# Weight tiles at other distances from the activations: one distance for the last feed-forward layer, a test series in the first, four in turn in the attention and the delta rule

## The chip, the cores and the metric

The program runs on one core of one Trainium2 chip. The metric is the device time of one execution in microseconds (us); 2737.4 us is the median of three runs of the kernel before. Where a profile is read, its times are those of one further execution, taken with the hardware profiler.

TensorE multiplies a stationary operand, which a weight load (LDWEIGHTS, the row PEld of the profile) puts into the array, with a moving operand that is streamed from SBUF. VectorE is DVE in the profile, ScalarE is ACT, GpSimd is POOL, and SP is the queue from which the weights' DMAs are issued.

## The reference

A trunk of two layers over 256 tokens of width 2048, all in float32:

```python
x = x + diff_attention(rms_norm(x, mixer_norm[0]), ...)   # 8 heads, two softmax maps a head
x = x + conv_ffn(rms_norm(x, ffn_norm[0]), ...)           # layer 0
x = x + gated_deltanet(rms_norm(x, mixer_norm[1]), ...)   # 16 q/k heads, 32 v heads, chunks of 64
x = x + conv_ffn(rms_norm(x, ffn_norm[1]), ...)           # layer 1

def conv_ffn(h, w_up, conv_w, conv_b, w_down):            # width 5504 = 43 * 128
    u = causal_dwconv(h @ w_up, conv_w) + conv_b
    val, gate = jnp.split(u, 2, axis=-1)
    return (jax.nn.silu(gate) * val) @ w_down
```

Nearly all arithmetic is in the projections: `h @ w_qkv` and `@ w_o` of the attention, `h @ w_in` and `@ w_out` of the delta rule, `h @ w_up` and `@ w_down` of the two feed-forward layers.

## The kernel before

**One projection.** Activations lie transposed in SBUF, 128 features by 256 tokens a tile, each as two parts (a rounded part and the rest, `a[:, 0]` and `a[:, 1]`), so that three products in the fast fp32r format stand for one in float32. `dense` (L98 to L118) computes one *block*: 256 output features over all `kt` input tiles. It takes the weights in chunks of four input tiles. `weights` (L77 to L90) brings a chunk by a DMA from SP's queue (`raw`), rounds it on ScalarE (`whi`, L88) and takes the rest on VectorE (`wlo`, L89). For each input tile and each half of the block, three matmuls follow at L115, L116 and L117: the stationary operand is 128 columns of `whi`, of `wlo`, of `whi` again, and the moving operand is a tile of 256 tokens. A block with 16 input tiles (`w_qk`, `w_o`, `w_up`, `w_in`) is 96 matmuls, one of `w_down` with 43 tiles is 258, one of `w_out` with 8 tiles is 48. `raw`, `whi` and `wlo` have three buffers each. `dense_tok` (L125) is the other form, with the weights as the moving operand, for `w_v` and `w_z`; the change leaves it as it is.

**The distance.** A buffer of `whi` or `wlo` is 128 elements longer than its data. `dense` starts the data `(place - x) % 128` elements into the buffer, where `place` stands for the activations' own position (HP, AP or OP) and `x` is an entry of `dist`, the first for `whi` and the second for `wlo`. So `x` is a distance between the addresses of moving and stationary operand, counted in elements of 4 bytes modulo 512 bytes: 51 is 204 bytes. Nothing but these addresses depends on `dist`. The default is (51, 51).

**Order.** The stages run one after the other: the attention (16 blocks `w_qk`, a query and a key block for each head; 4 of `w_v`; 8 of `w_o`), the feed-forward layer 0 (43 blocks `w_up`, then 8 of `w_down`), the delta rule (a gate block; four batches of heads, each with four "k" blocks, one "v" block, two of `w_z` and three "v" blocks; the eight `w_out` blocks of a batch come one batch later), and the feed-forward layer 1. TensorE works through the blocks in program order. In the mixers, `tick` (called after every chunk) puts the small matmuls of the attention and of the delta rule (tiles `mp`) between those of the projections; in the feed-forward layers only the norm's matmuls stand between them, in the first `w_up` block.

**Distances before.** The feed-forward layers hold series, block by block. `w_up` of layer 0 goes through 0 to 42, that of layer 1 through 43 to 63 and then through eleven pairs, 51 and one of 0, 16, 24, 32, 8, 4, 48, 60, 12, 36 and 51. `w_down` has pairs for `whi` and `wlo`, as the diff shows. All other projections have 51.

Of the kernel before, what the change touches and what calls it, by code (L numbers as in the profile page):

```python
# [19 lines left out]
KD = D // P  # L20
EPS = 1e-6
CK = 4
HP, AP, OP = 40, 48, 112
LNEXP = "natural_log_exp_and_others"


class Trunk:
# [38 lines left out]
    def mp(self):  # L66
        return self.mps.tile([P, 512], F32, tag="mp", name="mp")
# [9 lines left out]
    def weights(self, ap, d=(0, 0)):  # L77
# [4 lines left out]
        def tile_(tag, dt, bufs, room=0, d=0):  # L82
            t = self.wp.tile([P, CK * T + room], dt, tag=tag, name=tag, bufs=bufs)
            return t[:, d:d + nk * n].rearrange("p (k n) -> p k n", n=n)
# [15 lines left out]
    def dense(self, w, kt, acts, place, tiles=2, lead=0, dist=(51, 51)):  # L100
# [3 lines left out]
        ps = self.banks()  # L104
        for k0, nk in self.chunks(kt, CK, lead):
            hi, lo = self.weights(w[:, k0:k0 + nk, :], [(place - x) % P for x in dist])
# [18 lines left out]
    def dense_tok(self, w, kt, acts):  # L125

        nc = self.nc
        ps = self.banks()
        for k0, nk in self.chunks(kt, CK // 2):
            hi, lo = self.weights(w[:, k0:k0 + nk, :], (HP, HP))  # L130
# [118 lines left out]
    def ffn(self, w_up, w_down, nj, cols_ap, done, final=False):  # L249

        nc = self.nc
        self.spawn(self.norm_stat())
        with self.tc.tile_pool(name="fp", bufs=1) as fp:
            cols = fp.tile([P, 8 * nj + 64], F32, tag="fcols", name="fcols")[:, :8 * nj]
            cols = cols.rearrange("p (t h j) -> p t h j", t=4, h=2)
            nc.scalar.dma_start(cols, cols_ap)
            acts = []
            one = [(r, r) for r in range(64)]
            if final:
                ups = one[43:] + [one[r] for i in range(11) for r in (51, (0, 16, 24, 32, 8, 4, 48, 60, 12, 36, 51)[i])]  # L260
                downs = [(51, 51), (48, 48), (51, 19), (51, 35), (19, 51), (35, 51), (16, 51), (51, 16)]
            else:
                ups = one[:43]
                downs = [(51, 51), (51, 48), (48, 51), (51, 50), (51, 52), (51, 0), (48, 0), (51, 32)]
            rows = self.rows(fp.tile([P, nj * 2 * T + 8], F32R, tag="ac", name="ac"), nj, 0)
            for j in range(nj):
                ps = self.dense(w_up[j], KD, self.h_acts, HP, dist=ups[j])
                c = []
                u = fp.tile([P, 2, T], F32, tag="u", name="u", bufs=2)
                self.merge(ps, u)  # L270
                for half in range(2):
                    o = fp.tile([P, T], F32, tag=f"cv{half}", name="cv", bufs=2)
                    c4 = [cols[:, t, half, j:j + 1] for t in range(4)]
                    self.conv(o, u[:, half, :], c4[:3], c4[3])
                    c.append(o)
                nc.scalar.activation(c[1], c[1], AF.Silu)
                a = c[0]
                nc.vector.tensor_tensor(a, c[0], c[1], ALU.mult)
                ac = rows[j]
                self.split(ac, a)  # L280
                acts.append(ac)
            self.project(w_down, nj, lambda k: acts[k], AP, done, final, downs)

    def attention(self, w_qk, w_v, w_o, nh, dist_ap, ident_ap, qg, kg, lvec, sub, start, done, lambda_init):

        nc, mp = self.nc, self.mp
        with self.tc.tile_pool(name="at", bufs=1) as at:
            self.spawn(self.norm_stat(3))
            qgs = at.tile([P, 1], F32, tag="qgs", name="qgs")
# [3 lines left out]
            dist = at.tile([P, 384 + 72], F32, tag="dist", name="dist")[:, :384]  # L293
# [21 lines left out]
            def squares(r):  # L315
                sq = at.tile([P, 2, T], F32, tag="sq", name="sq", bufs=2)
                nc.scalar.square(sq, r)
                sp = at.tile([P, 2, 2, T], F32R, tag="sqp", name="sqp", bufs=3)
                self.split(sp, sq)
                return sp  # L320

            def normed(ps, gain):
                r = at.tile([P, 2, T], F32, tag="qkr", name="qkr", bufs=3)
                self.merge(ps, r)
                sq = squares(r)
                qn = at.tile([P, 2, T], F32, tag="qkn", name="qkn", bufs=4)

                def go():
                    yield
                    pn = mp()  # L330
                    self.total(pn, [sq])
                    ri = at.tile([P, 2, T], F32, tag="ri", name="ri", bufs=2)
                    self.rsqrt(ri, pn, P)
                    nc.vector.scalar_tensor_tensor(qn, r, gain, ri, ALU.mult, ALU.mult)

                return qn, go()
# [57 lines left out]
            aTs = []  # L394
            for h in range(nh):
                acts, lead = (self.h_acts, 0) if h else (start, 1)
                qn, go = normed(self.dense(w_qk[h], KD, acts, HP, lead=lead), qgs)
                self.spawn(go)
                kn, go = normed(self.dense(w_qk[nh + h], KD, self.h_acts, HP), kg)
                aT = at.tile([P, 384], F32, tag=f"aT{h}", name="aT")  # L400
                self.spawn(weigh(h, qn, kn, go, aT))
                aTs.append(aT)
# [14 lines left out]
    def gdn(self, w_gate, w_in, w_z, w_out, nb, hb, gate_ap, const_ap, hot_ap, conv_col, ng, done):  # L417
# [8 lines left out]
        nq = nb * hb  # L426
# [3 lines left out]
        with tc.tile_pool(name="gd", bufs=1) as gd:  # L430
# [20 lines left out]
            def lin(ps):  # L451
                u = gd.tile([P, 2, T], F32, tag="u", name="u", bufs=2)
                self.merge(ps, u)
                return u

            def convs(u, tiles):
                c = gd.tile([P, 2, T], F32, tag="cv", name="cv", bufs=4)
                for i in range(2):
                    self.conv(c[:, i, :], u[:, i, :], [conv_col(t, tiles[i]) for t in range(4)], None)
                nc.scalar.activation(c, c, AF.Silu)  # L460
                return c
# [204 lines left out]

            def out(b, acts):
                for blk in range(KD // 2):
                    ps = self.dense(w_out[b * (KD // 2) + blk], 2 * hb, lambda k: self.await_(acts, k), OP)
                    self.add_out(blk, ps, done if b == nb - 1 else None)  # L670

            pg = self.dense(w_gate, KD, self.h_acts, HP, tiles=1)
# [1 line left out]
            pend = None  # L674
            for b in range(nb):
                heads = range(b * hb, (b + 1) * hb)
                cc = gd.tile([P, 32, 32], F32, tag="s4", name="Cc", bufs=3)
                nc.gpsimd.memset(cc, 0.0)
                lqs, inv, acts, zts, vts = [], [], [], {}, {}
                groups = [range(i, i + gh) for i in range(0, hb, gh)]  # L680
                plan = [("k", i) for i in range(hb)] + [("v", 0)] + [("z", g) for g in range(len(groups))]
                for op, i in plan + [("v", i) for i in range(1, hb)]:
                    if op == "k":
                        hq = heads[i]
                        c = convs(lin(self.dense(w_in[hq * 2], KD, self.h_acts, HP)), (hq, nq + hq))
                        self.spawn(keys(hq, c, cc, 2 * i, lqs))
                        if i == hb - 1:
                            self.spawn(invert(cc, lqs, inv))
                    elif op == "z":
                        gr = groups[i]  # L690
                        zt = zts[i] = gd.tile([P, 2, gv, P], F32, tag="vz", name="zt", bufs=4)
                        ps = self.dense_tok(w_z[heads[gr[0]] // 2], KD, self.h_acts)
                        for t in range(2):
                            nc.scalar.activation(zt[:, t].rearrange(flat), ps[:, t, :], AF.Silu,
                                                 scale=self.rstdc[:, t:t + 1])
                    else:
                        gi = i // gh
                        gr = groups[gi]
                        if i == gr[0]:
                            vt = gd.tile([P, 2, gv, P], F32, tag="vz", name="vt", bufs=4)  # L700
                            ready = []
                            self.spawn(group(gi, gr, lqs, inv, vt, ready, zts, acts))
                        hq = heads[i]
                        c = convs(lin(self.dense(w_in[hq * 2 + 1], KD, self.h_acts, HP)),
                                  (2 * nq + 2 * hq, 2 * nq + 2 * hq + 1))
                        self.spawn(to_tokens(c, vt, 2 * (i - gr[0]), ready))
                if pend:
                    out(*pend)
                pend = (b, acts)
            out(*pend)  # L710

    def gates(self, gd, pg, nv, gp, ident, triu, res):
# [132 lines left out]
def trunk_kernel(tc, a, out):  # L845
    nc = tc.nc
    with ExitStack() as ctx:
# [3 lines left out]
        nc.sync.dma_start(cols[:, :KD], a["cols"][:, :KD])  # L851
        parts = t.chunks(KD, CK, 1)

# [58 lines left out]
```

## Time and profile before

| | |
|---|---|
| median of 3 runs (lowest, highest) | 2737.4 us (2737.03, 2738.95) |
| the profiled execution's own time | 2739.05 us |
| its span, first to last instruction | 2737.3 us |
| granted TensorE clock | 0.999 |
| `w_up` / `w_down` of layer 0 | 490.21 / 239.07 us |
| `w_up` / `w_down` of layer 1 | 483.28 / 240.51 us |
| attention's `w_qk` blocks with what lies between | 207.07 us |
| delta rule with `w_out` | 876.18 us |

How to read it: the stages' times are stretches of the span, cut where the first matmul of a stage starts. A matmul shows a modelled duration of about 280 ns in the profile though the next one starts some 113 to 125 ns after it, since they are pipelined. So what a block costs isn't read from the durations of its matmuls but from the time between starts: the stretch from the first matmul of a block to the first of the next, divided by its matmuls. This text calls it the block's *pace*. In a view of stretches, the number behind the x counts two or three more matmuls than the block has, because those of the neighbours reach into the stretch.

### The profile page before, as it was taken

To read this page: it belongs to the slowest core of one execution; us is meant where nothing else is said; L and a number is where in the kernel's file an instruction comes from. 1 tells how busy PE (TensorE), PEld (TensorE's weight loads), DVE (VectorE), ACT (ScalarE), POOL (GpSimd) and SP (SyncE) were. 2 spreads that over 40 slices of the span, in tenths; PEclk is the share of its full clock that TensorE was granted. 3 is DMA by queue.
4 is the path that set the end of the run, shared out by engine and by line. 5 is a ranking of instruction groups with operands and counts; after the bars stand their busy time and mean duration, and the time that the engine had idled before them with its cause. 6 is when DMAs were issued, how large, how long until landed. Compare 5 with 4: busy or idle time off the path is not lost.

```text
span 2737.3 us, 53669 instructions
## 1 busy us (share of the span) xinstructions
PE 2722.2 (99%) x22352; PEld 2651.4 (97%) x22352; DVE 1856.1 (68%) x2719; ACT 1453.3 (53%) x1994; POOL 118.0 (4%) x220
## 2 busy tenths in 40 slices
PE   8999999999999999999999999999999999999999
PEld 8998999999999999989989989989999999999999
DVE  7766667666666555689687787688676666675444
ACT  6555655555555444584664664574555555554333
POOL 0000000000000000021011011021000000000000
PEclk9999999999999999999999999999999999999999
DMA  6555565555555666545354454454455555666665
GB/s 207 168 165 175 159 200 184 185 186 186 185 185 185 196 190 187 182 155 176 115 171 145 148 170 147 154 165 160 145 189 187 186 189 188 187 192 196 200 194 157
DMA packets 135396, 481.62 MB, mean 176 GB/s; under 512 B 15344, under 2 KB 18416, under 8 KB 135152
## 3 DMA queue, kind: packets, MB, share of 16 engines
q1 hardware_dynamic: 134000, 475.57, 54.8%
q8 instruction: 175, 2.87, 0.4%
q10 hardware_dynamic: 1152, 2.61, 0.3%
q14 instruction: 69, 0.57, 0.1%
HBM read 476.03 MB, written 2.10 MB: 175 GB/s over the span
## 4 chain that ended last, share of the span: by engine, by line
PE 99%; ACT 0%; DVE 0%; DMA 0%; issue 0%; SPq 0%; DVEq 0%
PE ps L116 28%; PE ps L115 27%; PE ps L117 27%; PE ps L136 3%; PE ps L138 3%; PE ps L137 3%; PE mp L615 2%; PE mp L224 1%; PE mp L503 1%; PE mp L558 0%; PE mp L567 0%; PE mp L480 0%; PE mp L579 0%; PE mp L585 0%; PE mp L594 0%; PE mp L502 0%
## 5 line engine op out<-in xcount | busy, mean ns | idle before, releaser
L89 DVE TENSOR_TENSOR wlo<-raw,whi 128x1024 fp32r<-128x1024 f32 (+2 forms) x909 | 1108.7, 1221 | 683.6 <-ACT whi L88 678.8
L88 ACT CAST whi<-raw 128x1024 fp32r<-128x1024 f32 (+2 forms) x909 | 948.5, 1044 | 1093.1 <-PE ps L117 911.0
L115 PE MATMUL ps<-h,whi 128*128 128x256 f32 x4304 | 1208.6, 281 | 8.3 <-ACT h L150 6.0
L116 PE MATMUL ps<-h,wlo 128*128 128x256 f32 x4304 | 1210.2, 281 | 2.7 <-DVE wlo L89 2.7
L117 PE MATMUL ps<-h,whi 128*128 128x256 f32 x4304 | 1208.6, 281 | 0.0
L115 PEld LDWEIGHTS ps<-h,whi 128*128 128x128 f32 x4304 | 813.0, 189 | 11.1 <-ACT h L150 6.0
L116 PEld LDWEIGHTS ps<-h,wlo 128*128 128x128 f32 x4304 | 812.1, 189 | 6.5 <-DVE wlo L89 3.4
L117 PEld LDWEIGHTS ps<-h,whi 128*128 128x128 f32 x4304 | 812.0, 189 | 1.3
L116 PE MATMUL ps<-ac,wlo 128*128 128x256 f32 x1632 | 454.9, 279 | 0.0
L117 PE MATMUL ps<-ac,whi 128*128 128x256 f32 x1632 | 454.3, 279 | 0.0
L115 PE MATMUL ps<-ac,whi 128*128 128x256 f32 x1632 | 453.9, 278 | 0.0
L115 PEld LDWEIGHTS ps<-ac,whi 128*128 128x128 f32 x1632 | 307.0, 188 | 0.0
L117 PEld LDWEIGHTS ps<-ac,whi 128*128 128x128 f32 x1632 | 306.6, 188 | 0.0
L116 PEld LDWEIGHTS ps<-ac,wlo 128*128 128x128 f32 x1632 | 306.5, 188 | 0.0
L136 PE MATMUL ps<-whi,h 128*128 128x512 f32 x384 | 150.7, 393 | 0.0
L137 PE MATMUL ps<-wlo,h 128*128 128x512 f32 x384 | 150.0, 391 | 0.0
L138 PE MATMUL ps<-whi,h 128*128 128x512 f32 x384 | 149.9, 390 | 0.0
L115 PE MATMUL ps<-oc,whi 128*128 128x256 f32 x512 | 144.3, 282 | 0.0
L116 PE MATMUL ps<-oc,wlo 128*128 128x256 f32 x512 | 143.7, 281 | 0.0
L117 PE MATMUL ps<-oc,whi 128*128 128x256 f32 x512 | 143.6, 281 | 0.0
L205 DVE SCALAR_TENSOR_TENSOR cv<-u,fcols,cv 128x255 f32<-128x255 f32 (+1 forms) x344 | 142.9, 478 | 0.0
L123 DVE TENSOR_TENSOR u<-ps,rstd 128x512 f32<-128x512 f32 x118 | 81.5, 690 | 51.5 <-PE ps L117 51.2
(201 smaller groups left out, 2225.3 us busy)
## 6 DMA issues: line engine op xcount, KB each, us to landing
raw<-w_up SPq DMA_DIRECT2D x344, 512.0 KB, 4.1
raw<-w_down SPq DMA_DIRECT2D x160, 512.0 KB, 3.7
raw<-w_in SPq DMA_DIRECT2D x128, 512.0 KB, 4.2
raw<-w_z SPq DMA_DIRECT2D x64, 512.0 KB, 3.7
raw<-w_out SPq DMA_DIRECT2D x64, 512.0 KB, 3.6
raw<-w_qk SPq DMA_DIRECT2D x63, 512.0 KB, 3.9
raw<-w_v SPq DMA_DIRECT2D x32, 512.0 KB, 3.6
raw<-w_o SPq DMA_DIRECT2D x32, 512.0 KB, 4.3
```

Source lines behind the costliest of these rows:

```text
L88: nc.scalar.copy(hi, raw)
L89: nc.vector.tensor_tensor(lo, raw, hi.bitcast(F32), ALU.subtract)
L115: nc.tensor.matmul(o, hi[:, k, s], a[:, 0, :], start=first, stop=False)
L116: nc.tensor.matmul(o, lo[:, k, s], a[:, 0, :], start=False, stop=False)
L117: nc.tensor.matmul(o, hi[:, k, s], a[:, 1, :], start=False, stop=last)
L123: self.nc.vector.tensor_tensor(u, ps[:, :, :T], self.rstd.unsqueeze(1).to_broadcast([P, 2, T]), ALU.mult)
L136: nc.tensor.matmul(ps[:, c, :], ah, hi[:, k, :], start=first, stop=False)
L137: nc.tensor.matmul(ps[:, c, :], ah, lo[:, k, :], start=False, stop=False)
L138: nc.tensor.matmul(ps[:, c, :], al, hi[:, k, :], start=False, stop=last)
L205: nc.vector.scalar_tensor_tensor(out[:, j:], u[:, :T - j], taps[n - 1 - j], out[:, j:], ALU.mult, ALU.add)
L224: last = self.nc.tensor.matmul(out, self.onesr, p[:, j], start=i + j == 0, stop=i + j == n)
L615: nc.tensor.matmul(p[:, v, :], l(v), r[:, v, :], start=i == 0, stop=i == len(terms) - 1)
```

## The change

Only entries of `dist` change, so only the place of weight data within its buffers. Instructions, their order, sizes and buffers stay as they are.

```diff
+BEST = 13, 42, 45
...
-            one = [(r, r) for r in range(64)]
             if final:
-                ups = one[43:] + [one[r] for i in range(11) for r in (51, (0, 16, 24, 32, 8, 4, 48, 60, 12, 36, 51)[i])]
-                downs = [(51, 51), (48, 48), (51, 19), (51, 35), (19, 51), (35, 51), (16, 51), (51, 16)]
+                ups, downs = [(12, 12)] + [(51, 51)] * (nj - 1), [(51, 51)] * 8
             else:
-                ups = one[:43]
-                downs = [(51, 51), (51, 48), (48, 51), (51, 50), (51, 52), (51, 0), (48, 0), (51, 32)]
+                ups = [(x, x) for y in (0, 24, 37, 32, 17, 7, 48) for z in BEST for x in (y, z)] + [(13, 13)]
+                downs = [(x, x) for x in (13, 0, 13, 42, 0, 42, 45, 51)]
...
# attention, query and key blocks of head h
+                mine = 2 * ((BEST + (12,))[h % 4],)
-                qn, go = normed(self.dense(w_qk[h], KD, acts, HP, lead=lead), qgs)
+                qn, go = normed(self.dense(w_qk[h], KD, acts, HP, lead=lead, dist=mine), qgs)
...
# delta rule, batch b: "k" and "v" blocks (dist=mine) and the w_out blocks
+                mine = 2 * ((BEST + (12,))[b % 4],)
-                    ps = self.dense(w_out[b * (KD // 2) + blk], 2 * hb, lambda k: self.await_(acts, k), OP)
+                    ps = self.dense(w_out[b * (KD // 2) + blk], 2 * hb, lambda k: self.await_(acts, k), OP, dist=2 * ((BEST + (12,))[b % 4],))
```

Layer 1 has 12 in its first `w_up` block and 51 in all others and in `w_down`. Layer 0's `w_up` alternates: each of 0, 24, 37, 32, 17, 7 and 48 stands before each of 13, 42 and 45 once, and the 43rd block has 13 again; its `w_down` blocks have 13, 0, 13, 42, 0, 42, 45 and 51. Heads of the attention and batches of the delta rule take 13, 42, 45 and 12 in turn. `w_o`, the gate block, `w_v` and `w_z` keep what they had.

More of the change, by code (lines that the diff above doesn't have):

```diff
@@ L396, in attention @@
                 acts, lead = (self.h_acts, 0) if h else (start, 1)
-                qn, go = normed(self.dense(w_qk[h], KD, acts, HP, lead=lead), qgs)
+                mine = 2 * ((BEST + (12,))[h % 4],)
+                qn, go = normed(self.dense(w_qk[h], KD, acts, HP, lead=lead, dist=mine), qgs)
                 self.spawn(go)
-                kn, go = normed(self.dense(w_qk[nh + h], KD, self.h_acts, HP), kg)
+                kn, go = normed(self.dense(w_qk[nh + h], KD, self.h_acts, HP, dist=mine), kg)
                 aT = at.tile([P, 384], F32, tag=f"aT{h}", name="aT")
@@ L684, in gdn @@
                         hq = heads[i]
-                        c = convs(lin(self.dense(w_in[hq * 2], KD, self.h_acts, HP)), (hq, nq + hq))
+                        c = convs(lin(self.dense(w_in[hq * 2], KD, self.h_acts, HP, dist=mine)), (hq, nq + hq))
                         self.spawn(keys(hq, c, cc, 2 * i, lqs))
@@ L703, in gdn @@
                         hq = heads[i]
-                        c = convs(lin(self.dense(w_in[hq * 2 + 1], KD, self.h_acts, HP)),
+                        c = convs(lin(self.dense(w_in[hq * 2 + 1], KD, self.h_acts, HP, dist=mine)),
                                   (2 * nq + 2 * hq, 2 * nq + 2 * hq + 1))
```

## The prediction

> **What bounds the kernel now.** The page of the profile first: busy time and clock, the chain that ended last, then the groups of instructions.
>
> ```profile
> span 2737.3 us, 53669 instructions
> PE 2722.2 (99%) x22352; PEld 2651.4 (97%) x22352; DVE 1856.1 (68%) x2719; ACT 1453.3 (53%) x1994; POOL 118.0 (4%) x220
> PEclk9999999999999999999999999999999999999999
> L89 DVE TENSOR_TENSOR wlo<-raw,whi 128x1024 fp32r<-128x1024 f32 (+2 forms) x909 | 1108.7, 1221 | 683.6 <-ACT whi L88 678.8
> L116 PE MATMUL ps<-h,wlo 128*128 128x256 f32 x4304 | 1210.2, 281 | 2.7 <-DVE wlo L89 2.7
> ```
>
> TensorE has work in 99% of the span at the full granted clock, and its matmuls on `wlo` waited 2.7 us in all for the engine that makes it. So the weights come in time, and time can only come from the matmuls' pace. The views of stretches show the stages (stretch, its length, and each engine's busy time; in order: the attention's `w_qk`, layer 0 `w_up` and `w_down`, the delta rule, layer 1 `w_up` and `w_down`).
>
> ```profile
> 5.96:213.03 207.07, 203.01 (x1651) 199.85 (x1652) 152.20 (x243) 127.27 (x216) 0.00 (x0) 1.00 0.55 180
> 404.05:894.26 490.21, 490.21 (x4136) 490.16 (x4135) 338.26 (x476) 256.45 (x347) 0.00 (x0) 1.00 0.58 186
> 894.26:1133.33 239.07, 239.07 (x2067) 239.07 (x2065) 122.02 (x129) 101.89 (x120) 0.00 (x0) 1.00 0.60 185
> 1133.33:2009.51 876.18, 874.98 (x7046) 824.04 (x7045) 677.18 (x1135) 511.85 (x711) 117.81 (x216) 1.00 0.49 157
> 2009.51:2492.79 483.28, 483.28 (x4137) 483.23 (x4136) 337.59 (x476) 256.39 (x347) 0.00 (x0) 1.00 0.59 188
> 2492.79:2733.30 240.51, 240.51 (x2066) 240.44 (x2064) 110.48 (x100) 90.55 (x90) 0.00 (x0) 1.00 0.61 188
> ```
>
> The kernel before carries its own measurement, since its series gives each block another distance. The next stretches are single blocks of layer 1's `w_up`, for TensorE alone (length, busy time, matmuls, clock, DMA share, GB/s). In order: the first block (distance 43, with the norm's matmuls in it), 0, the 51 behind it, 24, the 51 behind it, 48 behind a 51, 12, the 51 behind it, and a 51 behind 36.
>
> ```profile
> 2009.51:2021.88 12.37, 11.96 (x98) 1.00 0.60 192
> 2258.84:2270.35 11.51, 11.51 (x98) 1.00 0.57 185
> 2270.35:2281.28 10.93, 10.93 (x98) 1.00 0.59 190
> 2303.05:2314.57 11.52, 11.52 (x99) 1.00 0.56 187
> 2314.57:2326.09 11.52, 11.52 (x99) 1.00 0.55 182
> 2393.39:2404.27 10.88, 10.88 (x99) 1.00 0.64 197
> 2437.42:2448.61 11.19, 11.19 (x98) 1.00 0.62 192
> 2448.61:2459.49 10.88, 10.88 (x98) 1.00 0.64 195
> 2471.01:2481.90 10.89, 10.89 (x98) 1.00 0.59 191
> ```
>
> The same 96 matmuls take 10.88 to 11.52 us, a pace of 113.3 to 120.0 ns, at one clock. Two things are read here. Distance matters: 0, 24 and 12 have paces of their own. And so does history: 51 ran at 10.88 to 10.93 behind 0, 12 and 36, but at 11.52 behind 24, for a whole block. So 51 has a quick gait and a lagging one that keeps itself up, and what stood before decides between them. Of eight entries into 51 from another distance in these pairs, the 24 above and a 32 ended slow, the first fast one being 0 and the last 36.
>
> [...]
>
> **The change part by part.** No instruction, DMA or wait is added, removed or moved. ScalarE and VectorE write the same bytes to shifted places. Their cover is the chunk of 24 matmuls, 2.72 us at the fast pace, against 1.22 us for `wlo`; in blocks that ran fast already the DMA moved 190 to 197 GB/s, so all queues have served that pace. If that cover went, the wait on `wlo` above would grow; 42 fast blocks in a row need no more than one does. Durations are those of the profiled execution, against its 2739.05 us (span 2737.3 and 1.75 around it), which is 1.65 above the median of the runs.
>
> Layer 1, `w_up`: 12 in the first block costs 11.19, and the norm's matmuls add what they added to the first block before: 12.37 against 11.51 to 11.52 without them, 0.87. Then 42 blocks with 51; the row behind a 12 says 10.88 at once, and I let it hold, since nothing interrupts these blocks (336 matmuls that bear on it stand at the end of the mixers' rows). At 10.89: 12.06 + 42 x 10.89 = 469.4, so -13.8.
>
> Layer 1, `w_down`, next two rows: (48, 48), entered from a quick block, and (51, 35).
>
> ```profile
> 2522.04:2551.28 29.24, 29.24 (x260) 1.00 0.66 204
> 2580.52:2611.33 30.81, 30.81 (x260) 1.00 0.63 196
> ```
>
> 29.24 is 258 at 113.3 ns. Eight such blocks are 233.9, so -6.6, if the quick gait is there when they begin.
>
> Layer 0, `w_up`: blocks of the old series with 7, 13, 17, 32, 37, 42 (all layer 0) and 45 (layer 1).
>
> ```profile
> 484.88:496.40 11.52, 11.52 (x99) 1.00 0.58 183
> 553.16:564.04 10.88, 10.88 (x98) 1.00 0.61 192
> 598.17:609.53 11.36, 11.36 (x99) 1.00 0.56 187
> 768.87:780.26 11.39, 11.39 (x99) 1.00 0.59 185
> 826.06:837.80 11.74, 11.74 (x99) 1.00 0.54 181
> 883.37:894.26 10.89, 10.89 (x98) 1.00 0.62 196
> 2033.28:2044.18 10.90, 10.90 (x99) 1.00 0.64 190
> ```
>
> 13, 42 and 45 ran fast, each entered once, from 12, 41 and 44. The six slow disturbers cost 3 x (11.51 + 11.52 + 11.74 + 11.39 + 11.36 + 11.52) = 207.1; 48 lies between 10.88 (entered from a quick block) and 11.52, and I take 10.88 twice and 11.52 once, 33.3. The 22 blocks of 13, 42 and 45 lie between 10.89 and 11.52. One fast entry each is less than 51 has shown, and 51 failed two of eight, so I take one entry in three as failing: 7 x 11.52 + 15 x 10.89 = 244.0. With 0.87 for the norm: 485.3, so -5.0. Ends: -10.0 with no failure (and 48 fast), +4.5 with all 21 failing (and 48 slow).
>
> Layer 0, `w_down`: six blocks at 29.24; 0 has no row at this length, and 258 x 11.51 / 96 = 30.9 for each of two. Sum 237.3, -1.8. A failing entry costs 258 x 0.63 / 96 = 1.7, and I take one: -0.1. Ends -1.8 and +8.6 (all eight at 30.96).
>
> Attention and delta rule: here small matmuls interrupt the blocks and throw the gait anew each time. First three rows: one head of the attention at 51 between interruptions (8.52, 5.28 and 7.72 us). Then a stretch of the last batch's "k" blocks, two "v" blocks behind `w_z`, and seven `w_out` blocks.
>
> ```profile
> 84.20:92.72 8.52, 8.52 (x73) 1.00 0.67 215
> 93.43:98.71 5.28, 5.28 (x44) 1.00 0.61 196
> 100.26:107.98 7.72, 7.72 (x70) 1.00 0.37 128
> 1758.18:1771.84 13.66, 13.66 (x117) 1.00 0.60 190
> 1859.50:1882.54 23.04, 23.04 (x193) 1.00 0.60 187
> 1971.43:2009.51 38.08, 38.08 (x338) 1.00 0.58 201
> ```
>
> 71 and 44 matmuls at 120.0 ns, 68 at 113.5; then 116 at 117.8 (a third gait of 51), 192 at 120.0, 336 at 113.3: the gaits of 51 hold for as long as nothing interrupts. A head has some 115 slow gaps: at most -0.78 us for each of the six with 13, 42 and 45, about -0.2 for the two with 12 (116.6 by its row); at worst +0.45 for each. I take -1.5 of -5.1 to +3.6. In the delta rule about nine "v" blocks, those behind `w_z`, stand at 11.52: 0.63 each, seven of them under the three new distances; two thirds cured give -2.9, and 12 gives -0.7 on two. The other 23 blocks recover mostly under 51; between -1.5 and +14.5 I take +2. The last `w_out` batch goes from 113.3 to 12's 116.6, 384 x 3.3 ns = +1.3, and the other 1152 matmuls, mostly fast now, cost at worst +7.7; I take +1.2. The mixers together: -0.6, ends -11 and +26.
>
> Sum: -13.8 - 6.6 - 5.0 - 0.1 - 0.6 = -26.1, so 2713.0 profiled and 2711 in the runs' median.
>
> **The rivals.** *51 locks into a lagging gait in layer 1* (the other side). The norm's matmuls interrupt the block of 12, so 12 may hand over in another phase than the one that it had when 51 took over fast. If 51 enters the gait of 120.0, nothing interrupts it for 50 blocks: 12.06 + 42 x 11.52 = 495.9 and 8 x 30.96 = 247.7, +12.6 and +7.2, and with the other terms 2737.4 + 19.8 - 5.7 = 2751.5. In that of 117.8, 42 x 11.31 and 8 x 30.39 give +3.8 and +2.6, 2738. It decides at one place, the second `w_up` block. For it: the 51 behind 24, and 192 matmuls at 120.0 in the mixers. Against: the row behind 12. Of the gain of 26, nothing is left when 26 of these 40 us return, so when two thirds of the 50 blocks run at 120.
>
> *The new distances are fast only beside the neighbours they were seen with.* Then layer 0 and the mixers lose while layer 1 gains: -20.4 + 4.5 + 8.6 and +5 to +26 in the mixers, 2735 to 2756 at its full size; half of it with the mixers unchanged gives 2723. For it: single entries, read out of a series of 64. Against: 51 was found in the same series and recovered in six entries of eight.
>
> *The distance does nothing by itself* and only history does: the stages keep their mean paces, 2737. Against it: behind a fast 51, 48 kept 10.88, while 0 and 12, also behind a 51, took 11.51 and 11.19. [...]
>
> **How the numbers follow.** Forecast case, layer 1 fast and layer 0 about as taken: 0.80, with a range of its own of 2699 to 2723. Locked: 0.07 at 2751, and 0.04 at 2738. New distances bad: 0.06, 2723 to 2745. No effect: 0.03. The lower end, 2698, is the layers' terms with no failure (-13.8 - 6.6 - 10.0 - 1.8 = -32.2) and two thirds of the mixers' best case, -7, together 2739.05 - 1.65 - 39.2. The upper end, 2731, takes in the milder half of the bad distances. Within 0.2% (5.5 us, about what a measurement of this kernel can tell from no change) lie the 117.8 lock, no effect and a part of the bad distances: 0.08. Slower: 0.09. Faster: 0.83.
>
> **What would show it.** The profile after should show layer 1's `w_up` near 469 and `w_down` near 234, with blocks of 10.88 from the second on; layer 0's alternation with blocks of 13, 42 and 45 at either 10.9 or a slow pace, whole blocks through; "v" blocks behind `w_z` at 10.9 in some batches; `w_out` of the last batch near 5.6 a block where it was 5.44. Layer 1's blocks at 11.5 would make the prediction wrong by their count, and a growing wait on `wlo` or on DMA would mean that the cover was taken too thick.

## The result, and the profile after

The changed kernel takes 2715.3 us in the median of four runs (2714.4 to 2716.8), against 2738.2 for the kernel before: ratio 0.9917, interval 0.9899 to 0.9934. The forecast was 2711 and a gain of 26; the gain is 22.9. The profiled execution has a span of 2713.3 us against 2737.3.

The page of the profile after, the rows that answer to those of before (`wlo` is now made at L90 and used at L117):

```profile
span 2713.3 us, 53669 instructions
PE 2699.1 (99%) x22352; PEld 2628.1 (97%) x22352; DVE 1852.9 (68%) x2719; ACT 1453.5 (54%) x1994; POOL 118.0 (4%) x220
L117 PE MATMUL ps<-h,wlo 128*128 128x256 f32 x4304 | 1202.1, 279 | 2.7 <-DVE wlo L90 2.7
```

The same number of instructions, and the same 2.7 us of waiting for `wlo`: the weights keep up with the quicker pace, and nothing took the place of the time that went. The view of stretches, by stage (attention's `w_qk`, layer 0 `w_up` and `w_down`, delta rule, layer 1 `w_up` and `w_down`):

```profile
5.87:210.97 205.10, 201.68 (x1651) 198.52 (x1652) 152.52 (x243) 127.22 (x216) 0.00 (x0) 1.00 0.58 182
401.97:884.78 482.81, 482.81 (x4137) 482.76 (x4135) 336.86 (x476) 256.62 (x347) 0.00 (x0) 1.00 0.62 189
884.78:1128.16 243.38, 243.38 (x2066) 243.38 (x2065) 122.02 (x129) 101.50 (x120) 0.00 (x0) 1.00 0.62 182
1128.16:2006.29 878.13, 877.01 (x7046) 825.93 (x7045) 677.59 (x1135) 512.21 (x711) 117.81 (x216) 1.00 0.51 157
2006.29:2475.38 469.09, 469.09 (x4137) 469.04 (x4136) 335.08 (x476) 256.28 (x347) 0.00 (x0) 1.00 0.64 194
2475.38:2709.32 233.94, 233.94 (x2066) 233.90 (x2064) 110.48 (x100) 90.76 (x90) 0.00 (x0) 1.00 0.66 193
```

Taken from the stretches of before: attention -2.0, layer 0 `w_up` -7.4 and `w_down` +4.3, delta rule +2.0, layer 1 `w_up` -14.2 and `w_down` -6.6, together -23.9 of the span's -24.0. So nearly nine tenths of the sum, 20.8, come from the last layer; the first layer gives 3.1 in its two stages, and the mixers cancel.

Layer 1's `w_up`, TensorE alone (length, busy time, matmuls, clock, DMA share, GB/s): the block of 12, the first block of 51, and the 41 blocks behind it.

```profile
2006.29:2018.38 12.09, 11.68 (x99) 1.00 0.60 193
2018.38:2029.29 10.91, 10.91 (x98) 1.00 0.60 190
2029.29:2475.38 446.09, 446.09 (x3939) 1.00 0.65 194
```

41 x 96 matmuls in 446.09 us are 113.3 ns each: once 51 is in its quick gait and nothing interrupts it, it stays there for 446 us. Layer 0's alternation is the counterpart. In order: 13, 42 and 45 behind 0; 13 behind 37.

```profile
414.36:426.18 11.82, 11.82 (x99) 1.00 0.55 177
437.69:448.89 11.20, 11.20 (x99) 1.00 0.60 188
460.41:471.31 10.90, 10.90 (x99) 1.00 0.61 189
550.01:561.53 11.52, 11.52 (x98) 1.00 0.60 183
```

The three distances differ: 45 came into 113.3 ns from all seven disturbers, 42 from six, 13 from three only (24, 17 and 48). Behind 0, 13 has a gait of 123 ns, above anything that it had shown before. Layer 0's `w_down` shows it again (13, 0, then the fourth block, 42 behind a 13, and the sixth, 42 behind 0; the third block, 13 again, took 31.80):

```profile
884.78:916.59 31.81, 31.81 (x261) 1.00 0.61 177
916.59:947.54 30.95, 30.95 (x260) 1.00 0.62 181
979.34:1008.58 29.24, 29.24 (x260) 1.00 0.65 187
1039.54:1069.65 30.11, 30.11 (x261) 1.00 0.65 187
```

In the delta rule, the two "v" blocks behind `w_z` in the batches with 13, 42 and 12 (23.04 before; 45 took 21.77), and the last batch's eight `w_out` blocks at 12:

```profile
1251.69:1275.36 23.67, 23.67 (x194) 1.00 0.59 182
1425.82:1447.60 21.78, 21.78 (x193) 1.00 0.60 177
1857.17:1879.57 22.40, 22.40 (x193) 1.00 0.61 189
1961.49:2006.29 44.80, 44.80 (x386) 1.00 0.60 195
```

42 and 45 come out of the lagging gait that held 51 there; 13 falls deeper; 12 keeps its constant 116.7 ns in both places, better than 120 and worse than 113.3.

### The profile page after: what moved, and what is told of

Its sections match the earlier page's. It is cut to its first block, busy times and chain, and to the rows that moved or that the text cites. A ratio compares the mean times of both kernels' runs of the same rounds, so it can differ in the third digit from the quotient of the medians.

```text
span 2713.3 us, 53669 instructions
## 1 busy us (share of the span) xinstructions
PE 2699.1 (99%) x22352; PEld 2628.1 (97%) x22352; DVE 1852.9 (68%) x2719; ACT 1453.5 (54%) x1994; POOL 118.0 (4%) x220
## 4 chain that ended last, share of the span: by engine, by line
PE 99%; ACT 0%; DVE 0%; DMA 0%; issue 0%; ACTq 0%; SPq 0%; DVEq 0%
PE ps L117 27%; PE ps L116 27%; PE ps L118 27%; PE ps L137 3%; PE ps L138 3%; PE ps L139 3%; PE mp L615 2%; PE mp L225 1%; PE mp L503 1%; PE mp L558 0%; PE mp L567 0%; PE mp L480 0%; PE mp L585 0%; PE mp L579 0%; PE mp L594 0%; PE mp L502 0%
## 5 line engine op out<-in xcount | busy, mean ns | idle before, releaser
L90 DVE TENSOR_TENSOR wlo<-raw,whi 128x1024 fp32r<-128x1024 f32 (+2 forms) x909 | 1110.0, 1222 | 670.0 <-ACT whi L89 666.6
L117 PE MATMUL ps<-h,wlo 128*128 128x256 f32 x4304 | 1202.1, 279 | 2.7 <-DVE wlo L90 2.7
L117 PEld LDWEIGHTS ps<-h,wlo 128*128 128x128 f32 x4304 | 811.8, 189 | 6.5 <-DVE wlo L90 3.4
L117 PE MATMUL ps<-ac,wlo 128*128 128x256 f32 x1632 | 453.6, 278 | 0.0
L117 PEld LDWEIGHTS ps<-ac,wlo 128*128 128x128 f32 x1632 | 307.5, 188 | 0.0
L117 PE MATMUL ps<-oc,wlo 128*128 128x256 f32 x512 | 143.7, 281 | 0.0
```

The lines of the kernel that those rows point to most:

```text
L90: nc.vector.tensor_tensor(lo, raw, hi.bitcast(F32), ALU.subtract)
L117: nc.tensor.matmul(o, lo[:, k, s], a[:, 0, :], start=False, stop=False)
```

## The experiments

The theory to be tested: the pace of a block is set by the distance *and* by the gait in which the block is entered; a gait keeps itself up until another distance or an interruption throws it. The rivals: the address alone decides; history alone decides; absolute places in SBUF count rather than the distance. Ratios are against the kernel before, timed on the same chip.

**A lagging stretch on purpose.** Layer 1's `w_up` gets 24 and 32 between its blocks of 51.

```diff
-                ups, downs = [(12, 12)] + [(51, 51)] * (nj - 1), [(51, 51)] * 8
+                ups = [(x, x) for x in [12, 51, 24] + [51] * 13 + [12] + [51] * 10 + [32] + [51] * 15]
+                downs = [(51, 51)] * 8
```

> The changed kernel with layer 1's first feed-forward projection at 12, 51, 24, then 51 thirteen times, 12, 51 ten times, 32, and 51 fifteen times; w_down stays at 51. Theory (history decides the gait of 51, and without an interruption a gait keeps itself up): 51 behind 24 and behind 32 runs at 120.0 ns, 11.52 us a block, through all thirteen and all fifteen blocks, at 113.3 ns (10.88 us) behind the two 12s; if the lagging gait also survives the switch to w_down, its eight blocks take 30.96 us each. Sum against the changed kernel's 2715.3: 28 x 0.64 + about 1.4 for 24, 32 and the second 12 = +19.3, and +13.8 in w_down: 2735 with the switch freeing it, 2748 without. Rival (a lagging stretch ends by itself within a block or two, and the address alone sets the pace): at most +3, 2718.

Measured: 2724.1 us, ratio 0.9945 (0.9930 to 0.9960). The stretches behind the 24, in order: thirteen blocks of 51, 12, ten of 51, 32, fifteen of 51.

```profile
2042.25:2192.01 149.76, 149.76 (x1251) 1.00 0.60 183
2192.01:2203.21 11.20, 11.20 (x99) 1.00 0.60 186
2203.21:2312.05 108.84, 108.84 (x963) 1.00 0.65 194
2312.05:2323.43 11.38, 11.38 (x98) 1.00 0.61 187
2323.43:2486.65 163.22, 163.22 (x1442) 1.00 0.65 194
```

149.76 us for 1248 matmuls are 120.0 ns: the same 51 that runs 446 us at 113.3 in the changed kernel runs 150 us at 120.0, and no block of the thirteen leaves. One block of 12 frees it: the ten behind it take 108.84 us, 113.4 ns a matmul. So the address alone doesn't decide. The expected second lock behind 32 did not come, and with it not the one in `w_down`: 32 itself ran at 11.38 here, entered from a quick 51, while the 32 of the kernel before that handed over a lagging 51 ran at 11.52, entered from a lagging one. By this pair, history reaches back over more than one block.

**The same, with interruptions.** Ahead of blocks 6, 9 and 12 (counted from 0), inside the thirteen, float32 matmuls into an unused PSUM tile:

```diff
+                for i in range({6: 1, 9: 3, 12: 2}.get(j, 0) if final else 0):
+                    extra = self.mp()
+                    nc.tensor.matmul(extra[:, :T], self.ones, self.x[:, i, :], start=True, stop=True)
                 ps = self.dense(w_up[j], KD, self.h_acts, HP, dist=ups[j])
```

> The kernel with 12, 51, 24, 51 ... in layer 1, with extra float32 matmuls (ones by a tile of x, into a PSUM tile that nobody reads) ahead of the blocks 6 (one), 9 (three) and 12 (two), inside the thirteen blocks that ran at 120.0 ns. Theory (an interruption throws the gait anew, and 51 takes up 113.3 ns after most of them): behind at least one of the three the blocks go to 10.88 us with no change of any address, w_up of layer 1 between 478.9 - 10 x 0.64 and 478.9 - 4 x 0.64, plus some 1.4 for six extra matmuls: 474 to 478. Rival (the lagging gait is tied to the addresses reached behind 24, and an interruption does nothing): all thirteen stay at 11.52 and w_up takes 480.3.

Measured: 2725.5 us, with `w_up` at 479.6. Only three of the six extra matmuls ran where they were meant to: the first three ran early, inside the stage's first block, so nothing stands ahead of block 6. One ran ahead of block 9 and two ahead of block 12, as the timeline shows (start, duration; a float32 matmul runs as two here):

```profile
2111.48 0.59 PE L269 MATMUL mp<-x,ones 128*128 128x256 f32 x2
2144.60 1.03 PE L269 MATMUL mp<-x,ones 128*128 128x256 f32 x4
```

The stretches of blocks 6 to 8 (with the one at its end), 9, 10 to 11 (with the two at its end) and 12 to 15:

```profile
2076.93:2111.73 34.80, 34.72 (x291) 1.00 0.60 183
2111.73:2122.84 11.11, 11.11 (x97) 1.00 0.60 186
2122.84:2145.28 22.44, 21.93 (x195) 1.00 0.62 191
2145.28:2191.55 46.27, 46.27 (x385) 1.00 0.60 182
```

Blocks 6 to 8 ran at 120.0 (34.56 for three blocks, 0.24 for the extra one). That one matmul freed the gait: 11.11 for the block in which it turned, then 21.76 for two blocks with 0.68 for the extra ones. Those two threw it back to 120.0 for four blocks. Blocks 9 to 11 have the addresses of the run before, in which they took 11.52 each, so the address alone is refuted a second time. The gain and the cost cancel, 479.6 against 478.9; the expected 474 to 478 assumed that a freed gait would last.

**Everything at one distance.** `ups`, `downs`, `mine` and the defaults all become 51, 45, 13 or 48 (the lines show 45); both `w_up` stages then begin without a 12.

```diff
-BEST = 13, 42, 45
+BEST = 45, 45, 45
...
-    def dense(self, w, kt, acts, place, tiles=2, lead=0, dist=(51, 51)):
+    def dense(self, w, kt, acts, place, tiles=2, lead=0, dist=(45, 45)):
...
-                ups, downs = [(12, 12)] + [(51, 51)] * (nj - 1), [(51, 51)] * 8
+                ups, downs = [(45, 45)] * nj, [(45, 45)] * 8
...
-                mine = 2 * ((BEST + (12,))[h % 4],)
+                mine = 2 * ((BEST + (45,))[h % 4],)
```

> 51 for every projection, also in both layers' first w_up block (no 12 and no disturbers). Theory (51 recovers from most interruptions, the norm's matmuls in the first block among them, and then holds): both w_up at 12.0 + 42 x 10.88 = 469, both w_down at 234, attention and delta rule as in the kernel before (207 and 876): 2738.2 - 21.2 - 5.1 - 14.2 - 6.6 = 2691. Rival (12 is needed to bring 51 into its quick gait after the norm's matmuls): each layer that stays at 120.0 costs 27 in w_up and up to 14 in w_down, so 2718 to 2732 with one and 2745 to 2773 with both.

Measured: 2690.8 us, ratio 0.9822 (0.9805 to 0.9838). Attention, layer 0 `w_up` (layer 1's takes the same 468.82) and delta rule:

```profile
5.97:212.61 206.64, 190.32 (x1537) 1.00 0.57 180
403.62:872.44 468.82, 468.19 (x4130) 1.00 0.65 194
1106.38:1982.73 876.35, 749.07 (x5426) 1.00 0.51 157
```

Both layers run quick, so 12 is not needed behind the norm's matmuls, and the mixers stand where they stood before.

> 45 for every projection. In the changed kernel 45 entered the quick gait in all seven of its blocks in layer 0 and behind most interruptions of the mixers. Theory (each distance has its own rate of return after an interruption, and 45's is the best): feed-forward layers as with 51 everywhere (469 and 234 twice), a head of the attention at 24.4 against 25.2 (about -6), a batch of w_in at 104.6 against 106.7 (-8 for four), w_out about -1: 2691 - 15 = 2676. Rival (the rate of return belongs to the place of the interruption, not to the distance): the mixers as with 51, 2691; and if 45 leaves its gait at a switch of stage, +14 for a w_down, up to 2705.

Measured: 2680.6 us, ratio 0.9786 (0.9772 to 0.9801). Attention and delta rule:

```profile
5.37:208.49 203.12, 185.90 (x1536) 1.00 0.60 184
1102.37:1975.30 872.93, 745.42 (x5427) 0.99 0.52 158
```

The feed-forward layers are those of 51 to 0.1 us. The attention is 3.5 shorter and the delta rule 3.4: 45 returns from interruptions where 51 lags, though by about half of what was expected, and not everywhere: the first batch's four "k" blocks took 52.9 against 51.5. A part of the shortfall is not the distance's. In the delta rule the profiled execution of 45 has four stretches of some 3.4 us in which the granted clock is 0.50, that of 51 has two, and the two more cost about 3 us (the last fence of this section shows some of these blocks). This is the best of the versions here, level with the last one below, and ahead of the kernel before and of the changed one.

> 13 for every projection: the distance whose blocks my estimate put between 113.3 and 120.0 and which ran at 123.3 in three stages. Theory (13 has a lagging gait of its own at 123.3, and the switch to w_down or an interruption throws it there more often than 51): if the norm's interruption leaves 13 at 123.3, w_up takes 43 x 11.83 = 509 in that layer, else 468.8; both w_down at 8 x 31.8 = 254 if the switch alone does it. Sum against 51 everywhere (2691): +40 for the two w_down alone, 2731, up to 2811 with both w_up, and the mixers +5 to +10 more. Rival (123.3 came from what stood before, 0 or w_z, and not from 13): feed-forward layers as with 51, 2691 to 2700.

Measured: 2788.4 us, ratio 1.0187 (1.0158 to 1.0217). `w_up` and `w_down` of layer 0 and of layer 1:

```profile
411.58:908.05 496.47, 495.84 (x4131) 1.00 0.59 183
908.05:1162.59 254.54, 254.54 (x2067) 1.00 0.60 174
2052.44:2548.65 496.21, 495.80 (x4130) 1.00 0.59 183
2548.65:2782.58 233.93, 233.93 (x2066) 1.00 0.66 193
```

13 has three gaits that hold for whole stages: 123.3 ns (254.54 for 2064 matmuls), 120.0 in both `w_up`, and 113.3 in layer 1's `w_down`, where the same eight blocks of the same form take 20.6 us less than in layer 0. I had expected 468.8 or 509 for a `w_up` and the same fate for both `w_down`; neither held. Both `w_down` were entered from a `w_up` at 120.0 and at the same distance, so the gait of the blocks before does not decide alone what comes out of a switch of stage; what else does stays open.

> 48 for every projection: the weights then start on a multiple of 32 bytes as the activations do, which 13, 42, 45 and 51 do not. Theory (a distance has gaits of its own, and which one it takes is thrown by the interruptions): 48 has 113.3, seen behind quick blocks, and 117.8, seen for a whole block when it came from 47; so each layer's w_up takes 469 or 486 and each w_down 234 or 243, by its first block alone, and the time is 2691 to 2750. Rival (what matters is that both operands stand on lines of 32 bytes): 48 runs at 113.3 behind every interruption, w_up 468.8 twice, the mixers better than with 45, 2680 or less.

Measured: 2716.9 us, ratio 0.9917 (0.9897 to 0.9937). `w_up` and `w_down` of layer 0; those of layer 1 are equal to 0.01 us:

```profile
405.84:874.61 468.77, 468.14 (x4130) 1.00 0.65 194
874.61:1117.71 243.10, 243.10 (x2067) 1.00 0.63 183
```

48 runs quick in both `w_up` and at 117.8 in both `w_down`, two of the values that the theory allowed. At 48 the weights, too, start on a multiple of 32 bytes, and that does not keep it quick.

**The place of the activations.** The normed activations and all weights that meet them move together by 5, 8 or 4 elements; every distance stays as in the changed kernel.

```diff
-HP, AP, OP = 40, 48, 112
+HP, AP, OP = 45, 48, 112
...
-        self.place(0)
+        self.place(5)
```

> The changed kernel with the normed activations and all weights that meet them moved by 5 elements (20 bytes) together, so that every distance stays as it was and every address of these stages changes. Theory (only the difference of the two addresses counts): each block of w_qk, w_up and w_in has the pace that it has in the changed kernel, to 0.1 us, and the time is 2715.3 within 2. Rival (the absolute place of the weights or of the activations counts, their place in a 16- or 64-byte line for instance): the blocks of 13, 42, 45 and 51 fall to 116 to 120 ns as the neighbours of those distances do, layer 1's w_up goes from 469 to about 483 to 496, and the time to 2730 or more.

Measured: 2795.3 us, ratio 1.0203 (1.0188 to 1.0218). Both forms of the expectation missed it; the rival came nearer. The second block of `w_z` in the first batch, then layer 1's `w_up` and its `w_down`, whose activations did not move:

```profile
1260.69:1283.30 22.61, 22.61 (x97) 1.00 0.62 187
2054.82:2555.26 500.44, 500.03 (x4130) 1.00 0.60 182
2555.26:2789.20 233.94, 233.94 (x2066) 1.00 0.66 193
```

`w_up` runs at 121 ns throughout (469.09 in the changed kernel), at the same distances, and its `w_down` is untouched. `w_z`, whose moving operand is the weights, shifted too, takes 22.61 where the changed kernel has 21.76. So the theory that the difference of the addresses is all was wrong: with the moving operand 20 bytes off a multiple of 32, the same distances cost 7 to 9 ns a matmul more in these two stages. The move shifted both operands. That the weights' own place does not explain it follows from layer 0's `w_up`: the weights of 45, 42 and 48 now stand where, within 32 bytes, those of 48, 45 and 51 had stood and run at 113.3 to 113.6 ns, and yet no block of that stage ran below 120.0 ns.

> As the shift by 5 elements, but by 8 (32 bytes), so that the activations stand on a multiple of 32 bytes again (their tile starts at byte 33440; 5 elements put it at 33460). Theory, second form (the distance counts, and so does the moving operand's place within a line of at most 32 bytes): w_up of layer 1 at 469 and the time back at 2715 within 3. Rival (any move of the activations away from their old place costs, or the line has 64 bytes, and 33440 was the good half): w_up of layer 1 stays near 500 and the time near 2795.

Measured: 2711.0 us, ratio 0.9905 (0.9876 to 0.9933); layer 0 and layer 1 `w_up`, then the first block of layer 0's `w_down`:

```profile
402.70:885.50 482.80, 482.17 (x4130) 1.00 0.62 189
1999.76:2468.84 469.08, 468.67 (x4131) 1.00 0.65 194
885.50:914.74 29.24, 29.24 (x260) 1.00 0.65 187
```

Moved by 32 bytes, both `w_up` have the changed kernel's time to 0.02 us (482.81 and 469.09), though all addresses differ and layer 0 alternates between ten distances. At these two places of the moving operand, both on a multiple of 32 bytes, nothing but the distance and the history shows in the times of these stages. It is not so at the switch to `w_down`: its own addresses did not move and the blocks ahead of it had their old pace, but its first block of 13 took 29.24 where the changed kernel has 31.81.

> The same move by 4 elements (16 bytes): a multiple of 16 bytes, but not of 32. If the line has 16 bytes, as the time of the move by 8; if it has 32 bytes, w_up of layer 1 near 500 (121 ns) and the time near 2795, as the move by 5.

Measured: 2753.8 us, ratio 1.0063 (1.0040 to 1.0086); layer 1 `w_up`:

```profile
2022.46:2514.06 491.60, 491.19 (x4130) 1.00 0.60 185
```

118.9 ns, between the two, so neither form of the expectation came: 51 did not keep its 113.3 ns at 16 bytes off a multiple of 32, but lost less there than at 20 bytes off (121 ns). Nor does it hold for every distance. In the same execution 42, in the three "v" blocks of the second batch, and 48, in a block of layer 0's `w_up`, ran at 113.4 and 113.9 ns:

```profile
1437.44:1470.09 32.65, 32.65 (x290) 1.00 0.63 191
841.32:852.25 10.93, 10.93 (x99) 1.00 0.62 190
```

So the moving operand's place counts together with the distance: the move by 16 bytes cost 5.6 ns a matmul at 51 and nothing at 42. A line of 16 or of 32 bytes, the expectation's two cases, is not shown.

**Distances by stage.**

```diff
# against the changed kernel; all other places have 45, as above
-                    ps = self.dense(w_out[b * (KD // 2) + blk], 2 * hb, lambda k: self.await_(acts, k), OP, dist=2 * ((BEST + (12,))[b % 4],))
+                    ps = self.dense(w_out[b * (KD // 2) + blk], 2 * hb, lambda k: self.await_(acts, k), OP, dist=2 * ((45, 42, 51, 45)[b % 4],))
...
# delta rule, batch b
-                mine = 2 * ((BEST + (12,))[b % 4],)
+                mine = 2 * ((45, 42, 45, 45)[b % 4],)
```

> 45 everywhere, but 42 for w_in and w_out of the delta rule's second batch and 51 for w_out of the third, chosen from the stages' times in the runs so far (w_in of the second batch 117.2 with 42 against 119.4 with 45; w_out of the second 66.0 with 42 against 66.9, of the third 65.3 to 65.4 against 66.9). Theory (a distance returns differently from each interruption, and what a batch showed in one kernel it shows again, since its interruptions are the same): -2.2 - 1.0 - 1.5 against 45 everywhere, 2676 of 2680.6. Rival (each interruption meets the matmuls at another moment once the stretch before has changed, so that the choice by stage does not carry over): within 2 of 2680.6, to either side.

Measured: 2681.4 us, ratio 0.9786 (0.9770 to 0.9803), the same as 45 everywhere, which is the rival's time. `w_out` of the second batch gained its 1.0, but that of the third stayed at 67.0, and `w_in` of the second took 118.7 where 117.2 was expected. The rows give another reason than the rival's. First blocks of `w_out`: in the second batch 45 (its run) and 42 (this one), in the third 45 (its run), 51 (this one) and 51 in the run with 51 everywhere; the clock is the number behind the matmuls.

```profile
1649.98:1660.43 10.45, 7.28 (x50) 0.84 0.33 102
1648.85:1657.66 8.81, 5.72 (x51) 1.00 0.33 111
1864.86:1875.30 10.44, 7.35 (x51) 0.84 0.32 104
1862.78:1873.24 10.46, 7.34 (x50) 0.84 0.33 105
1873.78:1882.60 8.82, 5.73 (x51) 1.00 0.35 113
```

The block takes 8.8 us at the full clock and 10.4 to 10.5 when a stretch of half clock falls into it. These stretches come and go between executions: in the third batch of the two lagging-stretch kernels, whose code is the same up to there, the block took 10.46 at 0.84 in the first and 8.84 at 1.00 in the second. The 1.0 and 1.5 of `w_out` on which the choice rested were this clock, not the distance, and the `w_in` with 117.2 had no such stretch, where this one and the 119.4 of 45 had one each. Whether a choice by stage carries over is therefore still open.

## Why the prediction was right, and where its terms were off

**What bounds it, and no cover lost.** Right. TensorE's share stays 99%, and the wait for `wlo` stays 2.7 us while DMA carries 194 GB/s in layer 1's `w_up`.

**Layer 1, -13.8 and -6.6.** Measured -14.2 and -6.6. The two gaits are shown: the lagging one was produced on purpose behind 24, in two kernels, at 120.0 ns and so at the rival's price of 0.64 us a block, and it ended by another distance or by an interruption. The rival's worry, that 12 must hand over in the right phase, is answered for 51 and 45: both came out of the norm's interruption without a 12. For 13, which stayed at 120.0 in both `w_up`, the worry would have been right. The prediction's count of entries was short: the pairs hold ten entries into 51 from another distance, not eight, and the two left out, behind 16 and 48, were quick.

**Layer 0 `w_up`, -5.0.** Measured -7.4. I let seven entries of 21 fail; five did (13 behind 0, 37, 32 and 7; 42 behind 0), and all three blocks of 48 were quick. The rate was near, but one rate for three distances was the wrong form: four failures in seven, one in seven, none in seven. The upper end of this term was added up wrong: by its own rows it is +5.2 and not +4.5.

**Layer 0 `w_down`, -0.1.** Measured +4.3, the step that failed. It took 120.0 as the slowest gait that a good distance can have, from rows of 51, and so 30.96 as the worst block. 13 has one at 123.3, and both its blocks took it: 31.81 and 31.80, 5.1 us above two quick ones. 42 behind 0 added 0.9. The stated worst case for all eight, +8.6, was too mild for the same reason. That the whole sum came within 2.2 us of the measured 23.9 is in part luck: this miss of 4.4 and the 2.4 in `w_up` have opposite signs.

**Mixers, -0.6.** Measured 0.0: attention -2.0 (taken -1.5), delta rule +2.0 (taken +0.9). The parts that rested on a row came as worked out: 12 in the last `w_out`, +1.2 (44.80 against 43.56 before) where +1.3 was forecast, and 42, 45 and 12 out of the 120.0 behind `w_z`. What was missed is 13 again, which made the first batch's "v" blocks 0.6 longer where they were thought cured. The split is no finer than the clock allows: with the same code in the mixers, the delta rule took 878.1 here, 876.8 in the first of the two lagging-stretch kernels and 875.3 in the second, with two, one and none of the stretches at half clock; the kernel before had two.

**The rival of distance without effect** is refuted: changing the common place by 32 bytes left both `w_up` as they were, while the distance alone took layer 0's `w_up` from 468.8 us (45 everywhere) to 496.5 (13 everywhere), and the whole from 2680.6 to 2788.4.

What stays open: why the pace follows the addresses of the two operands. The runs show that it changes with the difference of these addresses (layer 0's `w_up` took 468.8 us at 45 and 496.5 at 13), with a move of both by 16 or 20 bytes at the same difference (113.3 to 118.9 and 121 ns at 51) and with what ran before (113.3 or 120.0 ns for 51 at the same addresses), not by what cause.

## What to carry to other kernels

Before a matmul-bound kernel is called finished, the time between starts should be read block by block: equal matmuls at one clock ran here at paces from 113.3 to 123.3 ns. Put the moving operand on a multiple of 32 bytes, where 42, 45, 48 and 51 all ran at 113.3 to 113.6 ns in whole blocks here, then try distances between the weights' and the activations' addresses, and judge a distance by how it comes back from interruptions and not by one quick block; a series that enters each candidate from several others tells that, and a scan does not. Where a stage shows a constant lagging pace, one block at another distance or a single extra matmul may free it, and the next one may throw it back: here a block of 12 and one float32 matmul each took 51 from 120.0 ns to the quick gait, and two more such matmuls returned it to 120.0. Compare the granted clock before two stages of different executions are compared: here a stretch at half clock, 1.6 us in a `w_out` block, looked like the gain of a distance.

## What the runs showed of the hardware

Matmuls with 128 x 256 moving elements in fp32r ran, at the full granted clock, at 113.3, 116.7, 117.8, 120.0 and 123.3 ns from start to start, each held over whole blocks or stages. The same distance can have three of these (13: 113.3, 120.0 and 123.3), and in the `w_up` stages which one it had went with what ran before; at the switch to `w_down` 13 came out at 123.3 and at 113.3 behind the same 120.0. At 51, a move of both operands by 20 bytes raised 113.3 to 121 ns and one by 16 bytes to 118.9, while 42 and 48 ran at 113.4 and 113.9 after the move by 16; a move by 32 bytes left both `w_up` equal to 0.02 us. In the mixers the granted clock fell to 0.50 for some 3.4 us at a time, at none to four places of the delta rule, which made a `w_out` block 1.6 us longer.
